# Order of ScalarE and VectorE in the compression stage, and where weight splits stand in it

## The chip, the cores and the metric

The kernel runs on one core of a Trainium2 chip. The metric is the device time of one execution in microseconds. TensorE (PE) does the matrix products, ScalarE (ACT) and VectorE (DVE) copy, split and combine, GpSimd (POOL) helps, and SyncE (SP) issues nearly all DMA transfers.

## The reference, cut to what matters

One layer of a hybrid decoder block: RMSNorm, one wide input projection, an mLSTM branch and a sparse attention branch (NSA), merged and projected out. All in float32, for 512 tokens of width 1024. The changed part is the compression of keys and values for the NSA branch, with the rotary embedding (rope) of keys and queries around it:

```python
def _compress(kv, pos_emb, w1, w2):
    idx = jnp.arange(n_cmp)[:, None] * CMP_STRIDE + jnp.arange(CMP_BLOCK)[None, :]
    blocks = kv[:, idx] + pos_emb[None, None, :, None, :]
    blocks = jnp.moveaxis(blocks, 3, 1).reshape(B, G, n_cmp, CMP_BLOCK * dk)
    return jax.nn.gelu(blocks @ w1) @ w2
...
kc = _compress(kvh(p["n_kc"]), cmp_pos_k[l], cmp_w1_k[l], cmp_w2_k[l])
vc = _compress(kvh(p["n_vc"]), cmp_pos_v[l], cmp_w1_v[l], cmp_w2_v[l])
ks = _partial_rope(kvh(p["n_ks"]), positions).transpose(0, 2, 1, 3)
kw = _partial_rope(kvh(p["n_kw"]), positions).transpose(0, 2, 1, 3)
```

The compressed keys and values serve one softmax, the keys `ks` and `kw` two others. `_compress` works on 31 blocks, a width of 2048 and a hidden layer of 128: small products with a chain of small steps between them.

## The kernel before, in words

Every float32 product is made of three: both operands are split into a rounded high part (type fp32r) and a remainder, and high x high, high x low and low x high are summed. `split` (line 122) is two instructions: ScalarE copies to the high part, VectorE subtracts for the remainder. For a weight tile of 128 x 1024 they are called wh (ScalarE) and wl (VectorE) in the profile, and its raw tile is wr (three buffers; four of wh and wl each).

The input projection is cut into jobs of 128 columns. A job (`cols`) is 24 matmuls of 128x512 into one PSUM bank, "pp", on the normalised input hTh, hTl; then its `post` function reads the bank. The class `Stream` (line 156) deals these matmuls out one at a time: `stream.step(n)` writes n of them into the program, `stream.run()` finishes one job. They are the fillers that keep TensorE at work while other chains go on. When a job starts, `fetch` calls `weights` for a job further on (the stream holds two ahead): the transfer of wr, and in the kernel before the split at once.

The compression stage comes after three big products and ahead of the attention blocks. Its jobs, in order: the keys and the values to compress (their `post` is `blocks(i)`, line 799), two key jobs for rope (`kpost`), the first query job (`queries(0)`), then gate jobs (`gate_ab`) mixed with further query jobs.

- `blocks(i)`: loads W1 in two halves (wr) and W2; ScalarE copies the bank to Z (one buffer); GpSimd adds the position to overlapping windows, giving Xr; Xr is split into X and W1 into "w1t" (keys) or "yb" (values). In the kernel before all of that is written right there.
- `hidden(i)`: 16 matmuls of W1 and X into a "ps" bank, then ScalarE and VectorE add its halves: "both".
- `activated(i, both)`: one small product with "twice", then the tanh form of gelu in six small steps on ScalarE and VectorE: "u".
- `compress_k`, `compress_v`: one small product with W2, and small copies to KC or VC.
- `rope_a`, `rope_b`, `keys`, `query_heads`: ScalarE copies the bank to "rh"; SP sends four strips of 8 rows of rh into "rot"; VectorE multiplies ra = bank x Ct, rot = rot x St, and adds. For keys, ScalarE and VectorE then split into "k" (four transfers copy the halves to the other partitions); for a query, into two tiles "Th". The first scores of attention are products of k and Th.

What sets the order: the program is written once in Python, and a scheduler then places instructions on each engine by its own estimate of when each can start. An engine named in the set `ordered` keeps the order of the program instead; TensorE isn't in it in this stage. In the kernel before `ordered` is empty from the first big product up to line 1011, where ScalarE and VectorE join it until the attention blocks begin. Buffers (wr, wh, wl, Z, banks) are released by semaphores that the framework adds.

## Time and profile before

| | us |
|---|---|
| median of 3 runs | 606.8 (605.92 to 607.37) |
| profiled execution, its own time | 607.47 |
| its span, first to last instruction | 605.4 |
| TensorE busy in the span | 591.8 |
| VectorE / ScalarE / GpSimd busy | 485.8 / 350.5 / 81.9 |
| granted TensorE clock, mean | 0.994 |

Lines of a timeline read: start in us, duration in us, engine, source line, operation, result <- operands, shapes, count; in square brackets how long the engine was idle before it, and what released it. Nearly all instructions carry line 80, where a helper records them, so they are told apart by the names of their tiles. The compression stage takes from about 174 us (the start of the first job, keys to compress) to 220 us (the first scores).

### The profile page before, as it was taken

Reading aid. Unit: us, or ns where it says so; the run is one execution under the profiler, and the core shown is the slowest. Engines: PE = TensorE matmul, PEld = TensorE weight load, DVE = VectorE, ACT = ScalarE, POOL = GpSimd, SP = SyncE. Lnnn points to the kernel's source line nnn. Section 1 sums busy time; section 2 is a strip of 40 time slices with the busy share of each in tenths; the row PEclk is TensorE's granted clock in tenths of the full one; section 3 lists DMA queues with packets and bytes.
Section 4 is the critical chain, followed back from the end, with each engine's and each line's share of the span. In section 5 each row is a group of like instructions: output and inputs, shape, how many; then the busy total and the mean of one; then the engine's idle time right before and its main releaser. Section 6 shows DMA issues by size and latency. Waiting matters only on the chain.

```text
span 605.4 us, 8474 instructions
## 1 busy us (share of the span) xinstructions
PE 591.8 (98%) x2956; PEld 496.6 (82%) x2956; DVE 485.8 (80%) x901; ACT 350.5 (58%) x645; POOL 81.9 (14%) x136
## 2 busy tenths in 40 slices
PE   7999999999999899999999999999999999999995
PEld 6988888888887788888888888888887878888885
DVE  5879889597686688887876866889989897589975
ACT  5855546654457366657666665657665653434564
POOL 3100000000005011414324230001010101010121
PEclk9999999999999899999999999999999999999998
DMA  7956654402046644313132214423133153890633
GB/s 222 337 173 178 204 169 128 150 2 87 18 114 177 152 121 125 106 40 106 39 88 68 72 53 123 139 71 88 53 98 110 39 171 110 281 265 24 209 53 139
DMA packets 86740, 74.17 MB, mean 123 GB/s; under 512 B 5229, under 2 KB 69353, under 8 KB 86698
## 3 DMA queue, kind: packets, MB, share of 16 engines
q1 hardware_dynamic: 85400, 70.94, 39.3%
q0 software_dynamic: 1008, 2.36, 2.1%
q8 instruction: 23, 0.38, 0.3%
q10 hardware_dynamic: 290, 0.33, 0.2%
q14 instruction: 19, 0.16, 0.1%
HBM read 61.36 MB, written 8.45 MB: 115 GB/s over the span
## 4 chain that ended last, share of the span: by engine, by line
PE 57%; DVE 6%; ACT 2%; issue 2%; POOL 1%; POOLq 0%; DVEq 0%; ACTq 0%
PE pp L80 39%; PE ps L80 9%; PE pt L80 5%; PE po L80 4%; DVE u L80 2%; DVE wl L80 1%; DVE xo L80 1%; ACT Dm L80 1%; ACT qkh L80 0%; POOL Xr L824 0%; POOL rho L1364 0%; ACT num L80 0%; DVE yal L80 0%; ACT wh L80 0%; DVE num L80 0%
## 5 line engine op out<-in xcount | busy, mean ns | idle before, releaser
L80 PE MATMUL pp<-hTl,wh 128*128 128x512 f32 x352 | 142.7, 405 | 0.0
L80 PE MATMUL pp<-hTh,wh 128*128 128x512 f32 x352 | 139.3, 396 | 0.0
L80 PE MATMUL pp<-hTh,wl 128*128 128x512 f32 x352 | 139.0, 395 | 0.0
L80 DVE TENSOR_TENSOR wl<-wr,wh 128x1024 fp32r<-128x1024 f32 x56 | 69.2, 1239 | 12.0 <-ACT wh L80 11.8
L80 ACT ACTIVATE wh<-wr 128x1024 fp32r<-128x1024 f32 x56 | 58.5, 1059 | 33.3 <-PE pp L80 23.0
L80 PEld LDWEIGHTS pp<-hTh,wh 128*128 128x128 f32 x352 | 66.4, 189 | 12.8
L80 PEld LDWEIGHTS pp<-hTl,wh 128*128 128x128 f32 x352 | 66.6, 189 | 10.6
L80 PEld LDWEIGHTS pp<-hTh,wl 128*128 128x128 f32 x352 | 66.6, 189 | 10.6
L80 ACT ACTIVATE P<-P,st 128x128 f32<-128x128 f32 (+3 forms) x64 | 35.7, 558 | 28.5 <-DVE st L80 28.3
L1110 POOL TENSOR_SCALAR P<-P,st 128x128 f32<-128x128 f32 (+3 forms) x56 | 38.0, 696 | 91.7 <-DVE st L80 59.0
L80 DVE TENSOR_TENSOR wl<-T,wh 128x1024 fp32r<-128x1024 f32 x28 | 34.0, 1222 | 11.3 <-ACT wh L80 11.2
L80 DVE TENSOR_TENSOR wl<-R,wh 128x1024 fp32r<-128x1024 f32 x28 | 33.9, 1222 | 10.2 <-ACT wh L80 10.2
L80 DVE TENSOR_TENSOR ptl<-pt,pth 128x512 fp32r<-128x512 f32 (+1 forms) x64 | 30.9, 485 | 12.2 <-ACT pth L80 11.6
L80 ACT ACTIVATE wh<-T 128x1024 fp32r<-128x1024 f32 x28 | 29.4, 1056 | 18.3 <-PE pp L80 11.0
L80 ACT ACTIVATE pth<-pt 128x512 fp32r<-128x512 f32 (+1 forms) x64 | 27.5, 429 | 20.3 <-PE pt L80 20.0
L80 DVE SCALAR_TENSOR_TENSOR u<-pp,prm,u 128x511 f32<-128x511 f32 (+2 forms) x48 | 35.7, 743 | 2.6 <-ACT u L80 2.3
L80 ACT ACTIVATE wh<-R 128x1024 fp32r<-128x1024 f32 x28 | 29.1, 1056 | 12.4 <-PE pp L80 5.3
L80 DVE CUSTOM_DVE_ANT_0 P<-ps,cst 128x128 f32<-128x128 f32 (+3 forms) x64 | 30.6, 484 | 5.5 <-PE ps L80 5.3
L80 PE MATMUL ps<-k,Th 128*128 128x256 f32 (+2 forms) x112 | 28.6, 336 | 0.0
L80 PE MATMUL pt<-cst,P 128*128 128x128 f32 x160 | 27.9, 272 | 0.0
L80 PEld LDWEIGHTS pt<-cst,P 128*128 128x128 f32 x160 | 20.8, 140 | 7.1 <-DVE ptl L80 0.3
L80 PE MATMUL pp<-yah,wh 128*128 128x512 f32 x64 | 25.0, 390 | 0.0
(355 smaller groups left out, 1360.8 us busy)
## 6 DMA issues: line engine op xcount, KB each, us to landing
wr<-w_in SPq DMA_DIRECT2D x44, 512.0 KB
R<-w_in SPq DMA_DIRECT2D x24, 512.0 KB
gD<-sg SPq DMA_DIRECT2D x16, 256.0 KB
s<-gD SPq DMA_DIRECT2D x16, 256.0 KB
wr<-w_branch_a SPq DMA_DIRECT2D x8, 512.0 KB
R<-w_out SPq DMA_DIRECT2D x8, 512.0 KB
vD<-cq SPq DMA_DIRECT2D x8, 256.0 KB
wr<-vD SPq DMA_DIRECT2D x4, 512.0 KB
```

The source lines that it names most:

```text
L80: ins = fn(*args, **kw)
L1110: pool.tensor_scalar(pj, pj, st[:, 2, j : j + 1], 1.0, OP.mult, OP.mult)
```

## The change

ScalarE and VectorE join `ordered` after the first job of the stage instead of near its end. From then on `weights` doesn't split at once: it puts the split into a queue, `pending`, and a call of `prepare()` between two groups of fillers writes the oldest one into the program. The splits of W1 and X move from `blocks` into a function `pack`, which is called for the keys after the value job and for the values after `hidden(0)`; within it W1 now comes ahead of X. The calls of the stage are spread anew over the fillers: 16 matmuls between most steps of the small chains, 8 or 4 at others. The value compression moves behind the first query's heads. The stage has as many jobs, products and transfers as before.

```diff
+    pending = deque()
+    lazy = []
+
+    def prepare():
+        pending.popleft()()
...
-        split(raw, hi, lo, eng)
+        if lazy:
+            pending.append(lambda: split(raw, hi, lo, eng))
+        else:
+            split(raw, hi, lo, eng)
         return hi, lo
...
-                side_by_side(raw.rearrange("p j g n -> p j (g n)"), X, js)
-            for raw, js in zip(raws, halves_of_j):
-                side_by_side(raw, W1[i], js)
+                blocked.append(raw.rearrange("p j g n -> p j (g n)"))
             Xs.append(X)
+
+            def pack():
+                for dst, srcs in ((W1[i], raws), (X, blocked)):
+                    for src, js in zip(srcs, halves_of_j):
+                        side_by_side(src, dst, js)
+
+            packs.append(pack)
...
-    stream.run(3)
+    stream.run()
+    ordered.update(("act", "dve"))
+    lazy.append(True)
+    stream.run()
+    packs[0]()
+    stream.step(8)
+    prepare()
+    stream.step(8)
     u0 = hidden(0)
+    packs[1]()
     stream.step(16)
+    prepare()
+    stream.step(8)
     u0 = activated(0, u0)
-    stream.run()
+    stream.step(8)
     keys(0, rope_b(*roped.pop(("k", 0))))
     u1 = hidden(1)
+    stream.step(8)
+    prepare()
     compress_k(u0)
-    stream.step(16)
-    u1 = activated(1, u1)
-    stream.run()
+    stream.step(4)
+    keys(1, rope_b(*roped.pop(("k", 1))))
+    stream.step(8)
+    u1 = activated(1, u1)
+    stream.step(4)
-    keys(1, rope_b(*roped.pop(("k", 1))))
-    compress_v(u1)
-    ordered.update(("act", "dve"))
     first = query_turned(0)
     stream.step(4)
     query_heads(0, first)
-    stream.step(PRE_FILL)
+    prepare()
+    stream.step(8)
+    compress_v(u1)
+    lazy.clear()
+    stream.step(12)
     ordered.clear()
+    prepare()
```

How the instructions stand on the engines is shown at three places. In the names a number tells buffers of one kind apart, and the two kernels number them differently.

First, ScalarE at the start of the stage. pp_1631 is the bank of the key job, pp_1690 (before) and pp_1680 (now) that of the value job. Before:

```order
L80 ACTIVATE w1t_1604<-wr_1656 128x8x128
L80 ACTIVATE w1t_1604<-wr_1658 128x8x128
L80 ACTIVATE Z_1662<-pp_1631 64x256 x4
L80 ACTIVATE wh_1686<-wr_1684 128x1024
L80 ACTIVATE X0_1667<-Xr_1668 128x8x64
L80 ACTIVATE X0_1667<-Xr_1674 128x8x64
L80 ACTIVATE yb_1592<-wr_1715 128x8x128
L80 ACTIVATE Z_1721<-pp_1690 64x256 x4
```

Now:

```order
L80 ACTIVATE Z_1662<-pp_1631 64x256 x4
L80 ACTIVATE Z_1711<-pp_1680 64x256 x4
L80 ACTIVATE w1t_1604<-wr_1656 128x8x128
L80 ACTIVATE w1t_1604<-wr_1658 128x8x128
L80 ACTIVATE X0_1667<-Xr_1668 128x8x64
L80 ACTIVATE X0_1667<-Xr_1672 128x8x64
L80 ACTIVATE wh_1678<-wr_1676 128x1024
L80 ACTIVATE both_1773<-ps_1756 128x128
```

The copies of the value job's bank moved ahead of the splits of the keys' W1 and X, and one weight split is left ahead of "both".

Second, ScalarE where the first query is turned: pp_1894 (before) and pp_1884 (now) are the query job's bank, wh_1964, wh_2019 and wh_2093 the weights of jobs ahead, wh_1882 those of the job after the next one. Before:

```order
L80 ACTIVATE u1_1913<-ps_1911 128x64
L80 ACTIVATE k00_1609<-ra_1850 64x512
L80 ACTIVATE u21_1914<-u21_1914 128x64
L80 ACTIVATE rh_1930<-pp_1894 128x512
L80 ACTIVATE k10_1611<-ra_1850 64x512
L80 ACTIVATE VC0_1584<-ps_1948 32x64 x2
L80 ACTIVATE VC1_1585<-ps_1948 32x64 x2
L80 ACTIVATE wh_1964<-wr_1962 128x1024
L80 ACTIVATE wh_2019<-wr_2017 128x1024
L80 ACTIVATE wh_2093<-wr_2091 128x1024
L80 ACTIVATE Th_1973<-ra_1936 64x512
L80 ACTIVATE Th_1976<-ra_1936 64x512
```

Now:

```order
L80 ACTIVATE k00_1609<-ra_1848 64x512
L80 ACTIVATE k10_1611<-ra_1848 64x512
L80 ACTIVATE u1_1925<-ps_1923 128x64
L80 ACTIVATE u21_1926<-u21_1926 128x64
L80 ACTIVATE rh_1938<-pp_1884 128x512
L80 ACTIVATE Th_1957<-ra_1944 64x512
L80 ACTIVATE Th_1960<-ra_1944 64x512
L80 ACTIVATE wh_1882<-wr_1880 128x1024
L80 ACTIVATE VC0_1584<-ps_1973 32x64
L80 ACTIVATE wh_1950<-wr_1948 128x1024
```

The second keys and both steps of u1 moved ahead of rh, and the weight splits and VC behind Th.

Third, TensorE at the first scores, ps_2010. Before (pp_2023 is the second job after the query job, 24 matmuls of the first, pp_1968, lie ahead of it, and 7 of its own lie ahead of these rows):

```order
L80 MATMUL pp_2031<-KC0_1582,rh_1930 128x64 x4
L80 MATMUL pp_2023<-hTl_78,wh_1890 128x512
L80 MATMUL pp_2023<-hTh_77,wl_1891 128x512
L80 MATMUL pp_2023<-hTh_77,wh_1890 128x512
L80 MATMUL pp_2023<-hTl_78,wh_1890 128x512
L80 MATMUL pp_2023<-hTh_77,wl_1891 128x512
L80 MATMUL pp_2023<-hTh_77,wh_1890 128x512
L80 MATMUL pp_2023<-hTl_78,wh_1890 128x512
L80 MATMUL ps_2010<-k00_1609,Th_1973 128x256
L80 MATMUL ps_2010<-k01_1610,Th_1973 128x256
```

Now (pp_1952 is the first job after the query job, and this is its last matmul):

```order
L80 MATMUL pp_1952<-hTh_77,wl_1803 128x512
L80 MATMUL ps_1973<-w2t1_1608,u1_1925 64x64
L80 MATMUL ps_2010<-k00_1609,Th_1957 128x256
L80 MATMUL ps_2010<-k01_1610,Th_1957 128x256
L80 MATMUL pp_2023<-hTh_77,wh_1882 128x512
L80 MATMUL pp_2023<-hTl_78,wh_1882 128x512
L80 MATMUL pp_2031<-KC0_1582,rh_1938 128x64 x3
```

Between the query job and the first scores there were 24 + 14 fillers, and there are 24; the value product moved from the middle of the job after the query to its end.

## The prediction

> **What bounds the kernel now.** I read the page first, its busy line and three rows of its 40 slices.

> ```profile
> PE 591.8 (98%) x2956; PEld 496.6 (82%) x2956; DVE 485.8 (80%) x901; ACT 350.5 (58%) x645; POOL 81.9 (14%) x136
> PE   7999999999999899999999999999999999999995
> PEclk9999999999999899999999999999999999999998
> ```

> TensorE is busy for 591.8 of 605.4 us. What an edit can win is the 13.6 us in which it is idle, and the time in which its clock is low. Start and end hold most of the idle time; between them one slice, the fourteenth (197 to 212 us), has an 8 for PE and an 8 for its clock. The windows view splits it (columns: us, busy time of PE, PEld, DVE, ACT, POOL with instruction counts, clock, DMA share, GB/s).

> ```profile
> 0.00:30.00 30.00, 26.41 (x170) 23.93 (x171) 20.90 (x35) 21.10 (x38) 7.27 (x21) 1.00 0.89 279
> 179.14:184.58 5.44, 5.44 (x26) 4.50 (x24) 3.67 (x3) 3.76 (x7) 3.42 (x3) 1.00 0.41 110
> 195.75:198.34 2.59, 0.00 (x1) 0.00 (x1) 2.53 (x4) 1.14 (x2) 0.00 (x0) 1.00 0.75 209
> 199.00:202.40 3.40, 3.40 (x11) 2.71 (x10) 2.20 (x7) 0.66 (x3) 0.00 (x0) 0.50 0.86 213
> 600.00:605.40 5.40, 0.00 (x0) 0.00 (x0) 0.87 (x3) 1.51 (x3) 0.55 (x1) 0.66 0.52 194
> ```

> The start costs 3.6 us and the last slice 5.4; the change touches neither. In the compression stage TensorE stands still for 2.59 us, and then runs for 3.4 us at half clock (0.50), which loses 1.7 us more. So the stage offers 2.6 + 1.7 = 4.3 us and no more. The second row is one filler job: 24 matmuls in 5.44 us, 0.227 us each. The timeline of VectorE and TensorE tells what held it up:

> ```profile
> 191.64 2.09 DVE L80 TENSOR_TENSOR X<-Xr,X 128x512 fp32r<-128x512 f32 x2
> 193.99 2.36 DVE L80 TENSOR_TENSOR wl<-wr,wh 128x1024 fp32r<-128x1024 f32 x2 [0.26 <-ACT wh L80]
> 196.87 1.22 DVE L80 TENSOR_TENSOR wl<-wr,wh 128x1024 fp32r<-128x1024 f32 x1
> 198.00 0.29 DVE L80 TENSOR_TENSOR both<-ps,both 128x128 f32<-128x128 f32 x1
> 198.34 0.43 PE L80 MATMUL ps<-twice,both 128*128 128x64 f32 x2 [2.59 <-DVE both L80]
> ```

> The addition for "both" (0.29 us) stands behind three weight splits of filler jobs. Nothing else is late in the stage: after 198.34 TensorE has no gap up to the attention blocks.

> **What the change removes.** With both engines in program order and each split postponed to the middle of the job ahead, "both" of key and value have one split ahead of them instead of three, and 16 fillers between. The 2.59 us gap should go: minus 2.6 us. How the low clock goes with it is weighed below.

> **What it adds, step by step.** I walk through the new order with durations of these rows (ScalarE and VectorE; "xN" rows are whole groups):

> ```profile
> 178.42 2.01 ACT L80 ACTIVATE w1t<-wr 128x1024 fp32r<-128x1024 f32 x2 [1.65 <-DVE gate L80]
> 179.52 2.36 DVE L80 TENSOR_TENSOR w1t<-wr,w1t 128x1024 fp32r<-128x1024 f32 x2 [1.03 <-ACT w1t L80]
> 180.34 1.55 ACT L80 ACTIVATE Z<-pp 64x256 f32<-64x256 f32 x4
> 184.58 0.39 PE L80 MATMUL pp<-hTh,wh 128*128 128x512 f32 x1
> 184.97 1.36 ACT L80 ACTIVATE X<-Xr 128x512 fp32r<-128x512 f32 x2 [2.00 <-POOL Xr L824]
> 185.64 1.42 DVE L80 TENSOR_TENSOR X<-Xr,X 128x512 fp32r<-128x512 f32 x2 [1.32 <-ACT X L80]
> 190.02 2.08 PE L80 MATMUL ps<-w1t,X 128*128 128x256 f32 x16
> 199.07 0.23 DVE L80 TENSOR_TENSOR u<-u 128x64 f32<-128x64 f32 x1 [0.78 <-ACT u L80]
> 199.82 0.26 ACT L80 ACTIVATE u<-u 128x64 f32<-128x64 f32 x1 [0.78 <-DVE u L80]
> 202.53 1.27 ACT L80 ACTIVATE k<-ra 64x512 fp32r<-64x512 f32 x2
> 203.27 1.39 DVE L80 TENSOR_TENSOR k<-ra,k 64x512 fp32r<-64x512 f32 x2
> 205.02 0.20 DVE L80 COPY KC<-ps 64x32 f32<-64x32 f32 x1
> 205.47 0.19 DVE L80 COPY KC<-ps 64x32 f32<-64x32 f32 x1 [0.26 <-ACT KC L80]
> 207.37 0.55 SPq L890 DMA_DIRECT2D k<-k  x1
> ```

> First hidden layer. Up to 184.6 us both kernels run the same matmuls without a gap. The Z copies of the value job now stand ahead of the splits of W1 and X, and wait for that job's last matmul, 184.8. Z 1.55 gives 186.3; the first half of w1t 187.4; VectorE's two w1t remainders 189.7; the first X remainder 190.4. TensorE comes there after 23 fillers, 184.58 + 23 x 0.227 = 189.8: it waits 0.6 us. (Bounds: 0 if the semaphores come a little earlier, 1.3 with the whole of X.)

> Second hidden layer. The hidden layer takes 1.9 us, then come 1 + 16 fillers, the small product (0.3) and 8 more: 198.3. VectorE has "both" by 193, two yb remainders by 196.2, X by 197.6: in time. W1 of the values is fetched later than now (its buffers come free with the w1t remainders, 188.6 and 189.7); at the 209 GB/s above a 512 KB transfer takes 2.5 us, so at worst it lands at 194.7 and X is late by 0.5 us. I take 0.

> Activation and keys. ScalarE's rh copy of the second key job waits behind the tanh of u (200.4), which waits for X, ra and a split on VectorE (199.4); it ends at 201.0. VectorE then does ra, rot, ra (3 x 0.69, to 203.1), ScalarE two k (to 204.4), "both" (204.7) and a split (205.8). TensorE, with 8 + 14 fillers behind it, needs "both" at 205.5: ready at 205.4. It ends the query job at 206.25, and its next job's third matmul (206.7) waits for the split's remainder, 205.8 + 1.22 = 207.0: 0.3 us. That job, the last one with weights ready, ends at 212.0. Meanwhile: copies of KC to 207.6, rot and ra of the second keys to 209.0, two k on ScalarE to 210.3, u to 210.5, VectorE's k remainder to 211.0 and u to 211.8, tanh 212.0, two small steps 212.4. The value product waits for them 0.4 us and ends at 212.7.

> The query's rope is the step that decides. It follows in the rows of the kernel before like this, for both key jobs and the query job:

> ```profile
> 194.93 0.60 ACT L80 ACTIVATE rh<-pp 128x512 f32<-128x512 f32 x1
> 200.00 0.69 DVE L80 TENSOR_TENSOR rot<-rot,St 128x512 f32<-128x512 f32 x1 [0.21 <-DMA rot<-rh]
> 202.03 0.60 ACT L80 ACTIVATE rh<-pp 128x512 f32<-128x512 f32 x1 [1.96 <-PE pp L80]
> 206.84 0.69 DVE L80 TENSOR_TENSOR rot<-rot,St 128x512 f32<-128x512 f32 x1 [1.18 <-DMA rot<-rh]
> 210.20 0.60 ACT L80 ACTIVATE rh<-pp 128x512 f32<-128x512 f32 x1
> 210.82 3.54 SPq L770 DMA_DIRECT2D rot<-rh  x4
> 215.81 0.69 DVE L80 TENSOR_TENSOR rot<-rot,St 128x512 f32<-128x512 f32 x1 [1.22 <-DMA rot<-rh]
> 217.27 1.28 ACT L80 ACTIVATE Th<-ra 64x512 fp32r<-64x512 f32 x2 [0.25 <-DVE ra L80]
> 218.40 1.40 DVE L80 TENSOR_TENSOR Th<-ra,Th 64x512 fp32r<-64x512 f32 x2
> 220.03 0.63 PE L80 MATMUL ps<-k,Th 128*128 128x256 f32 x4
> ```

> From the end of rh to the rot multiplication: 4.5, 4.2 and 5.0 us, four small transfers issued one after another by SP; VectorE waits for them each time. From rh's start to the first score: 9.8 us here, in which TensorE did 38 fillers, since the weights of two jobs were split ahead of Th. In the new order the split of the next job stands behind both Th on ScalarE, so TensorE has 24 fillers after the query job and then nothing: neither the score nor a filler can start. The rh copy itself stands behind the second keys and u's tanh: 212.0. SP issues the second keys' four transfers ahead of rot's (0.55 us each, the last after VectorE's k remainder at 211.0), and is free by 212.6. Then 0.6 for rh, transfers 4.5, rot and ra 1.4, Th 0.63, its remainder 0.69: 219.8. TensorE waits from 212.7: **7.1 us**. Bounds: the least is rh at the very end of the query job, with the shortest transfer: 0.6 + 4.2 + 1.4 + 1.3 = 7.5 us against 24 fillers, 5.44: 2.1 us. The most is this walk with transfers of 5.0 and 1 us more of queueing ahead: 8.6. I take the walk, because program order holds rh behind the tanh whatever the engines do. The next job's first matmul then waits for its split, which ends 1.06 us after the second Th, 220.75, against scores done at 220.3: 0.45 us.

> Sum of new waits: 0.6 + 0.3 + 0.4 + 7.1 + 0.45 = 8.85 us, against 2.59 removed: plus 6.25.

> Clock. The low clock of now began at 199.0, 3.25 us after TensorE stopped, and ended 4.1 us after it resumed. After 7.1 us of standing still it is certainly low at the restart; if it recovers as above, within 0.9 to 4.3 us after the restart, it loses half of that, 0.45 to 2.1. I take 1.5, so that 1.7 goes and 1.5 comes: minus 0.2. The small waits bring no low clock: no run of low clock but this and the end shows in the slices. [...]

> After the scores. The four small splits and two copies of VC, and two more weight splits, now fall into the first blocks of attention. VectorE has little room there:

> ```profile
> 213.24 0.29 DVE L80 CAST VC<-VC 64x256 fp32r<-64x256 f32 x1
> 213.56 0.22 DVE L80 TENSOR_TENSOR VC<-ps,VC 32x64 fp32r<-32x64 f32 x1
> ```

> ```profile
> 220.00:230.00 10.00, 10.00 (x53) 8.40 (x52) 9.69 (x32) 6.78 (x19) 2.61 (x3) 1.00 0.73 204
> ```

> They bring it some 3.9 us of work (two splits 2.4, VC 4 x 0.22 + 2 x 0.29 = 1.5). Bounds 0 to 3.9; I take 0, because the fillers of the next two jobs cover TensorE and its half clock gives VectorE time; the 3.9 is the upper end of the range.

> Total: 6.25 - 0.2 = about 6.0 us. The profiled execution took 607.47 us for a span of 605.4 (2.1 around it), so it becomes 613.5; the median of the three runs is 606.8, 0.7 below it, and becomes **612.8 us**.

> **The rivals.** (1) The gap goes and the rope hardly costs: 2.1 us of waiting, too little for the clock to fall, and 4.3 won: 606.8 - 2.2 = 604.6. For it: the earlier gap was 2.59 and small waits elsewhere leave the clock alone. Against it: it needs rh to start when the query job ends, while two k copies that hang on the second rope's transfers, and two steps of u behind them, stand ahead of it on ScalarE. It wins as soon as the wait for Th is under about 3 us. (2) It balances: a wait of some 4 us with its low clock costs what it saves, 605.6 to 608.0; for that the second keys would have to be done 3 us sooner than in my walk, for example if their transfers land under the split ahead. (3) The backlog of VC and splits stops TensorE in the attention blocks too: 612.8 + 3.9 = 616.7. For it, VectorE at 9.69 of 10; against it, the fillers. That the change does nothing can be left out: the order of both engines is another.

> **How the numbers follow.** Forecast 0.72; (1) 0.08; (2) 0.07; (3) 0.13. About 0.2% (1.2 us) is what a measurement of this kernel can tell from no change. Faster 0.09, the same 0.06, slower 0.85. The range goes from a wait of some 3.5 us with its clock (3.6 us less than the walk's 7.1: 609.2, and 0.7 less for the small waits: 608.5) to just under the third case: 616.5.

> **What would show it.** Right: no wait at "twice, both"; a gap of 5 to 8.5 us of TensorE ahead of the first product of k and Th, released by VectorE's Th, with rot's transfers in the chain of waits, and clock 0.50 right behind it. Wrong: the first score without a wait, or rh of the query job within a microsecond of that job's last matmul. If the gap is there and the time isn't up, my belief that TensorE's order can't make it good later is wrong.

## The result: 1.45% slower, and the profile after

The changed kernel takes 615.77 us (median, 614.8 to 616.19), the kernel before beside it 607.03. The ratio is 1.0145, with a 95% interval of 1.013 to 1.0161: 8.7 us slower, where the prediction had 6.0 and a range that ends at 616.5. The profiled execution took 614.8 us for a span of 612.8.

Of the page of the changed kernel, these are the busy line and TensorE's two rows of the 40 slices:

```profile
PE 594.2 (97%) x2956; PEld 497.3 (81%) x2956; DVE 486.2 (79%) x901; ACT 350.8 (57%) x645; POOL 82.8 (14%) x136
PE   8999999999999869999999999999999999999995
PEclk9999999999999979999999999999999999999999
```

The hole of the fourteenth slice is now in the fifteenth (a 6), with a 7 for the clock beside it. The first 176 us of an execution differ by up to 1.25 us from one profile to the next, so I compare a stretch rather than dates: from the start of ScalarE's last step on zt, ahead of the stage, to the first product of lf in the attention blocks. Where two kernels' dates are compared below, they too are counted from that step. In the windows view (length, then busy time of PE, PEld, DVE, ACT, POOL, clock, DMA share, GB/s) the kernel before has for it

```profile
176.14:262.25 86.11, 83.52 (x425) 69.92 (x425) 66.22 (x155) 53.70 (x119) 22.21 (x31) 0.98 0.49 127
```

and the changed kernel, with the part at low clock that follows the long wait as the second row,

```profile
175.16:269.54 94.38, 84.86 (x426) 70.20 (x425) 66.53 (x154) 53.36 (x119) 21.45 (x30) 0.96 0.44 116
...
220.11:224.77 4.66, 4.45 (x14) 3.67 (x15) 4.15 (x11) 4.24 (x10) 0.56 (x1) 0.50 0.26 63
```

So the stretch is 8.27 us longer. The profiled executions themselves differ by 7.3 us (614.80 and 607.47), since the part ahead of the stretch was 0.98 us shorter in the changed kernel's; the medians differ by 8.7. TensorE's idle time in it went from 2.59 to 9.52 us, plus 6.93. The low clock cost half of 3.41 us before (1.7) and half of 4.66 now (2.3), plus 0.6. The last 0.7 lies in TensorE's busy time at full clock, and I can't place it for certain. An estimate: a matmul is shown 0.39 us long while they follow each other 0.227 apart, so each wait may be some 0.16 us longer than it is shown; with six waits instead of one that would be 0.8 us.

TensorE's timeline of the changed kernel shows where it stands still:

```profile
190.47 1.78 PE L80 MATMUL ps<-w1t,X 128*128 128x256 f32 x13 [1.50 <-issue]
...
205.70 0.43 PE L80 MATMUL ps<-twice,both 128*128 128x64 f32 x2
...
213.19 0.30 PE L80 MATMUL ps<-w2t,u 128*64 128x64 f32 x2 [0.69 <-ACT rh L80]
220.11 0.80 PE L80 MATMUL ps<-k,Th 128*128 128x256 f32 x2 [6.62 <-DVE Th L80]
221.12 0.79 PE L80 MATMUL pp<-hTh,wh 128*128 128x512 f32 x1 [0.21 <-ACT wh L80]
...
234.81 0.60 PE L80 MATMUL pp<-cst,sc 128*64 128x128 f32 x4 [0.39 <-DVE sc L80]
```

The old wait at "twice, both" is gone. The first product of w1t and X waits 1.50 us, and the view names nothing that released it ("issue"); the run pack_first below shows that it waits for the splits of W1 and X. The first score waits 6.62 us, released by VectorE's Th. The chain ahead of it, from ScalarE's, SP's and VectorE's timelines of the changed kernel:

```profile
209.35 1.29 ACT L80 ACTIVATE k<-ra 64x512 fp32r<-64x512 f32 x2 [1.71 <-DVE ra L80]
...
212.19 0.26 ACT L80 ACTIVATE u<-u 128x64 f32<-128x64 f32 x1 [1.31 <-DVE u L80]
212.41 0.60 ACT L80 ACTIVATE rh<-pp 128x512 f32<-128x512 f32 x1
...
213.04 2.76 SPq L779 DMA_DIRECT2D rot<-rh  x4
...
217.26 0.69 DVE L80 TENSOR_TENSOR rot<-rot,St 128x512 f32<-128x512 f32 x1 [3.52 <-DMA rot<-rh]
...
218.71 1.28 ACT L80 ACTIVATE Th<-ra 64x512 fp32r<-64x512 f32 x2 [5.70 <-DVE ra L80]
220.01 1.06 ACT L80 ACTIVATE wh<-wr 128x1024 fp32r<-128x1024 f32 x1
```

rh stands behind the second keys' k and the tanh of u, although the query job's last matmul ended at 206.65. ScalarE then waits 5.70 us for the rope. The split of the next job (wh, 220.01) could have run in that time, but in program order it comes after Th.

### The profile page after: what moved, and what is told of

It is laid out like the page before. It is cut to its first block, busy times and chain, and to the rows that moved or that the text cites. A ratio compares the mean times of both kernels' runs of the same rounds, so it can differ in the third digit from the quotient of the medians.

```text
span 612.8 us, 8481 instructions
## 1 busy us (share of the span) xinstructions
PE 594.2 (97%) x2956; PEld 497.3 (81%) x2956; DVE 486.2 (79%) x901; ACT 350.8 (57%) x645; POOL 82.8 (14%) x136
## 3 DMA queue, kind: packets, MB, share of 16 engines
q0 software_dynamic: 1008, 2.36, 2.1%
## 4 chain that ended last, share of the span: by engine, by line
PE 81%; DVE 8%; ACT 4%; issue 2%; DMA 2%; POOL 1%; SPq 1%; POOLq 0%; DVEq 0%; ACTq 0%
PE pp L80 47%; PE ps L80 19%; PE pt L80 11%; PE po L80 4%; DVE u L80 2%; DVE wl L80 2%; DVE xo L80 1%; DMA xt<-x 1%; ACT Dm L80 1%; DMA wr<-cmp_w_v 1%; SPq L779 1%; DMA rot<-rh 1%; ACT wh L80 1%; ACT qkh L80 0%; POOL rho L1395 0%
## 5 line engine op out<-in xcount | busy, mean ns | idle before, releaser
L80 PE MATMUL pp<-hTl,wh 128*128 128x512 f32 x352 | 142.6, 405 | 0.0
L80 PE MATMUL pp<-hTh,wh 128*128 128x512 f32 x352 | 139.4, 396 | 0.2 <-ACT wh L80 0.2
L80 PE MATMUL pp<-hTh,wl 128*128 128x512 f32 x352 | 138.8, 394 | 0.1
L80 DVE TENSOR_TENSOR wl<-wr,wh 128x1024 fp32r<-128x1024 f32 x56 | 69.4, 1239 | 12.0 <-ACT wh L80 11.6
L80 ACT ACTIVATE wh<-wr 128x1024 fp32r<-128x1024 f32 x56 | 58.9, 1058 | 33.0 <-PE pp L80 26.6
L80 PEld LDWEIGHTS pp<-hTh,wh 128*128 128x128 f32 x352 | 66.5, 189 | 13.2 <-ACT wh L80 0.5
L80 PEld LDWEIGHTS pp<-hTh,wl 128*128 128x128 f32 x352 | 66.6, 189 | 10.9 <-DVE wl L80 0.6
L80 PEld LDWEIGHTS pp<-hTl,wh 128*128 128x128 f32 x352 | 66.6, 189 | 10.6
L80 ACT ACTIVATE P<-P,st 128x128 f32<-128x128 f32 (+3 forms) x64 | 35.7, 558 | 30.3 <-DVE st L80 30.2
L1141 POOL TENSOR_SCALAR P<-P,st 128x128 f32<-128x128 f32 (+3 forms) x56 | 39.7, 727 | 90.6 <-DVE st L80 65.3
L80 DVE TENSOR_TENSOR wl<-T,wh 128x1024 fp32r<-128x1024 f32 x28 | 34.0, 1222 | 12.4 <-ACT wh L80 12.3
L80 DVE TENSOR_TENSOR wl<-R,wh 128x1024 fp32r<-128x1024 f32 x28 | 33.8, 1220 | 10.4 <-ACT wh L80 10.4
L80 DVE TENSOR_TENSOR ptl<-pt,pth 128x512 fp32r<-128x512 f32 (+1 forms) x64 | 30.9, 485 | 12.6 <-ACT pth L80 11.9
L80 ACT ACTIVATE wh<-T 128x1024 fp32r<-128x1024 f32 x28 | 29.4, 1056 | 18.3 <-PE pp L80 11.0
L80 ACT ACTIVATE pth<-pt 128x512 fp32r<-128x512 f32 (+1 forms) x64 | 27.5, 429 | 19.2 <-PE pt L80 18.8
L80 DVE SCALAR_TENSOR_TENSOR u<-pp,prm,u 128x511 f32<-128x511 f32 (+2 forms) x48 | 35.6, 742 | 2.6 <-ACT u L80 2.3
L80 ACT ACTIVATE wh<-R 128x1024 fp32r<-128x1024 f32 x28 | 29.1, 1056 | 13.5 <-PE pp L80 6.4
L80 PE MATMUL ps<-k,Th 128*128 128x256 f32 (+2 forms) x112 | 29.0, 340 | 6.6 <-DVE Th L80 6.6
L80 DVE CUSTOM_DVE_ANT_0 P<-ps,cst 128x128 f32<-128x128 f32 (+3 forms) x64 | 30.5, 481 | 5.4 <-PE ps L80 5.2
L80 PE MATMUL pt<-cst,P 128*128 128x128 f32 x160 | 28.1, 272 | 0.0
L80 PEld LDWEIGHTS pt<-cst,P 128*128 128x128 f32 x160 | 20.8, 140 | 7.0 <-DVE ptl L80 0.3
L80 PEld LDWEIGHTS ps<-k,Th 128*128 128x128 f32 x112 | 19.0, 191 | 7.8 <-DVE Th L80 6.8
```

Source lines behind the costliest of these rows:

```text
L80: ins = fn(*args, **kw)
L1141: pool.tensor_scalar(pj, pj, st[:, 2, j : j + 1], 1.0, OP.mult, OP.mult)
```

## The experiments

Times are medians, with the ratio to the kernel before that ran beside them; "stretch" is the length defined above, and "idle" TensorE's idle time in it.

| kernel | us | ratio (95%) | stretch | idle |
|---|---|---|---|---|
| before | 605.7 to 607.2 | | 86.11 | 2.59 |
| changed | 615.77 | 1.0145 (1.0130 to 1.0161) | 94.38 | 9.52 |
| split_ahead | 609.89 | 1.0051 (1.0032 to 1.0071) | 87.82 | 4.43 |
| idle_matmuls | 613.90 | 1.0122 (1.0101 to 1.0143) | 92.46 | 3.27 |
| order_alone | 604.61 | 0.9957 (0.9942 to 0.9972) | 83.74 | 1.28 |
| no_order | 605.39 | 0.9975 (0.9963 to 0.9986) | 84.80 | 2.44 |
| pack_first | 612.36 | 1.0114 (1.0092 to 1.0135) | 91.33 | 6.20 |
| query_first | 613.53 | 1.0126 (1.0108 to 1.0144) | 92.72 | 7.09 |
| value_later | 605.93 | 0.9987 (0.9974 to 1.0000) | 85.12 | 1.97 |
| both_moved | 605.72 | 0.9993 (0.9982 to 1.0003) | 84.63 | 1.79 |
| behind_th | 604.84 | 0.9971 (0.9956 to 0.9986) | 83.97 | 1.52 |
| half_idle | 615.65 | 1.0152 (1.0128 to 1.0177) | 94.85 | 6.53 |
| next_behind_th | 610.84 | 1.0072 (1.0045 to 1.0098) | 90.07 | 4.61 |
| past_u | 604.09 | 0.9954 (0.9940 to 0.9969) | 83.17 | 0.80 |

**split_ahead: the next job's split ahead of the query's rope.** The changed kernel with

```diff
     stream.step(4)
+    prepare()
     first = query_turned(0)
     stream.step(4)
     query_heads(0, first)
-    prepare()
```

> The changed kernel with one call moved: the split of the job that follows the query job is issued ahead of the query's rope instead of behind both Th. Theory (the first score has no filler to cover the rope): those 24 fillers now run while the four transfers of rot, the rope and Th are done, so the 6.62 us wait at the first product of k and Th falls below 1.5 us, the 0.50 clock at 220 us is gone, at most 1 us of waiting for the split itself comes, and the time is 615.8 - 6.6 - 2.3 + 0.5 = about 607.4 (606 to 609). Rival A (program order itself holds both engines back, so that a wait taken away at one place comes up at the next): 612 to 616, with a new wait of over 4 us in the same 15 us. Rival B (the work left over for VectorE in the first attention blocks is what costs): the wait shifts behind the first scores, 611 to 615.

The long wait and the low clock are gone, and the stretch is 6.6 us shorter; the time is just above the range expected. Of the idle time that is left, 2.7 us lie ahead of the scores (first hidden layer 1.52, value product 0.67, the split itself 0.52); what is new lies behind them. In the timelines of TensorE, VectorE and GpSimd of this kernel:

```profile
223.92 0.40 PE L80 MATMUL ps<-k,Th 128*128 128x256 f32 x2
...
228.87 0.33 PE L80 MATMUL pt<-cst,P 128*128 128x128 f32 x1 [1.47 <-POOL P L1114]
...
224.79 1.23 DVE L80 TENSOR_TENSOR wl<-wr,wh 128x1024 fp32r<-128x1024 f32 x1
226.05 0.21 DVE L80 TENSOR_TENSOR VC<-ps,VC 32x64 fp32r<-32x64 f32 x1
...
227.23 0.14 DVE L80 RECIPROCAL st<-st 128x1 f32<-128x1 f32 x1
227.30 1.19 DVE L80 TENSOR_TENSOR wl<-wr,wh 128x1024 fp32r<-128x1024 f32 x1
...
227.71 1.11 POOL L1114 TENSOR_SCALAR P<-P,st,gates 128x128 f32<-128x128 f32 x1 [38.88 <-ACT wh L80]
```

The first transposes of P wait 1.47 us for GpSimd. Its step reads P, st and gates, and starts 0.34 us after the reciprocal of st, which stands on VectorE behind a weight split and pieces of VC (the view names a wh of ScalarE, which the step doesn't read). The step then takes 1.11 us beside the next split's wl, where the same step takes 0.45 us in the kernel before. This is the backlog of the prediction's third rival: it was hidden in the changed kernel while TensorE was late anyway, and came out once it wasn't. Rival B named the right work but not its size: it is 1.5 us of the 8.7, not the whole. Rival A fell, since no wait of over 4 us took the place.

**idle_matmuls and half_idle: what the low clock costs by itself.** The changed kernel with matmuls written in front of the first score, 26 or 12 of them:

```diff
     compress_v(u1)
+    ordered.add("pe")
+    idle = PT()
+    for n in range(26):
+        pe.matmul(idle, hTh[:, 0, 0:128], hTh[:, 1, :], start=True, stop=True)
+    ordered.discard("pe")
```

> The changed kernel with 26 matmuls more, whose result nobody reads, on TensorE between the value product and the first score: 26 x 0.227 = 5.9 us, which lie in the 6.62 us wait. The first score can start no sooner. Theory (the low clock behind the wait costs 2.3 us by itself): TensorE stands still for under 1.5 us, no slice of low clock behind it, and the time is 615.8 - 2.3 = 613.5 (612.8 to 614.3). Rival (the low clock is free, since VectorE or the weights set the pace behind the wait): 615.8, within 0.6.

> The changed kernel with 12 matmuls in the wait at Th instead of 26, so that about 0.47 + 14 x 0.227 = 3.65 us of standing still are left. So far waits up to 1.5 us had no low clock, 2.59 us one stretch of 3.41 us at 0.50, and 4.89, 5.01 and 6.62 us one stretch of 6.83 us each. Theory (low clock comes in steps of 3.41 us, of which a longer wait takes more): one stretch of 3.41 us, of which 0.5 to 1.7 us are lost: 613.9 + 1.1 = 615.0 (614.2 to 615.8). Rival (the length is always two steps once a wait passes some 3 us): 6.83 us and 2.3 us or more lost: 616 to 617.

With 26, TensorE's timeline has

```profile
213.76 6.21 PE L80 MATMUL pt<-hTh 128*128 128x512 f32 x26
220.44 0.50 PE L80 MATMUL ps<-k,Th 128*128 128x256 f32 x2 [0.47 <-DVE Th L80]
```

and the clock stays at 1.00. The score starts no sooner (44.98 us after the start of the stretch, 44.95 in the changed kernel), and yet the stretch is 1.92 us shorter and the time, 613.90, is where the theory had it: the low clock is a cost of its own, a little less than the 2.33 counted. With 12, in the timeline and in a window at the low clock,

```profile
220.95 0.79 PE L80 MATMUL ps<-k,Th 128*128 128x256 f32 x2 [3.66 <-DVE Th L80]
...
220.95:226.88 5.93, 5.71 (x18) 4.74 (x19) 4.15 (x11) 4.26 (x10) 0.56 (x1) 0.50 0.42 111
```

a wait of 3.66 us is followed by 5.93 us at half clock, 3.0 us lost, more than after 6.62 us. The time fell in the range of the theory, but for a wrong reason: the low clock lasted two steps (6.83 us, of which 0.9 fell into the wait), as the rival had it. The rival's time was 0.4 us too high.

**order_alone: program order without postponed splits.** The kernel before with

```diff
     stream.run(3)
+    ordered.update(("act", "dve"))
     u0 = hidden(0)
...
     compress_v(u1)
-    ordered.update(("act", "dve"))
     first = query_turned(0)
```

> The kernel before with one part of the change alone: ScalarE and VectorE in program order from the first hidden layer on; splits are issued when a job's weights are fetched, as before, and the rest of the stage is as before. Theory (not the order costs, but that the split of the next job was put behind Th): both splits stand ahead of Th, so no long wait at the first score; and the addition for both of the key stands ahead of the split fetched after it, so that the 2.59 us wait falls below 1 us with its low clock: 607.0 - 1.6 - 1.7 = 603.7 to 605.5. Rival A (program order itself costs): a wait of over 3 us at the rope of the query or of the second keys, 610 or more. Rival C (the 2.59 us are no order matter but the amount of split work in that stretch): 606.5 to 607.5.

It is 0.43% faster than before. From VectorE's and ScalarE's timelines of this kernel:

```profile
195.58 0.28 DVE L80 TENSOR_TENSOR both<-ps,both 128x128 f32<-128x128 f32 x1
195.78 1.21 DVE L80 TENSOR_TENSOR wl<-wr,wh 128x1024 fp32r<-128x1024 f32 x1
...
213.69 2.96 ACT L80 ACTIVATE wh<-wr 128x1024 fp32r<-128x1024 f32 x3
216.55 1.27 ACT L80 ACTIVATE Th<-ra 64x512 fp32r<-64x512 f32 x2
```

"both" stands behind one weight split instead of three, and its wait is 0.32 us instead of 2.59. Three splits stand ahead of Th, so the score has fillers and waits for nothing. Program order is not what made the change slow; on its own it takes away the old wait and its low clock.

**no_order: postponed splits without program order.** The changed kernel with

```diff
     stream.run()
-    ordered.update(("act", "dve"))
     lazy.append(True)
```

> The changed kernel without its program order for the stage (nor the one that the kernel before has around Th): postponed splits, packs and the closer steps alone, ScalarE's and VectorE's instructions arranged by the scheduler. Theory: the scheduler puts the split of the next job ahead of Th, so the first score has fillers ahead of it; some wait at both of up to 1.2 us stays; no low clock: 602.5 to 606. Rival D (postponing the splits costs by itself, whatever the order): a wait of over 4 us for a split or for Th, 611 or more.

This too is faster than before, by 0.25%. The scheduler puts a split between rh and Th, in ScalarE's timeline:

```profile
208.32 0.58 ACT L80 ACTIVATE rh<-pp 128x512 f32<-128x512 f32 x1
...
212.42 1.06 ACT L80 ACTIVATE wh<-wr 128x1024 fp32r<-128x1024 f32 x1 [0.42 <-PE pp L80]
...
218.35 1.28 ACT L80 ACTIVATE Th<-ra 64x512 fp32r<-64x512 f32 x2 [0.85 <-DVE ra L80]
```

From rh to Th it takes 10.0 us here, longer than in the changed kernel (6.3), and there is no wait at the first score. TensorE's idle time, 2.44 us, is nearly what it was before (2.59), but it is spread over waits of 1.01 us at most, and no low clock follows: that is what this half gains. So each half of the change gains; together they lose, because program order keeps the postponed split where it was written.

**behind_th and next_behind_th: is the split behind Th enough?** Both add the queue of postponed splits to the kernel of order_alone and use it around the query alone. In behind_th,

```diff
     first = query_turned(0)
+    lazy.append(True)
     stream.step(4)
+    lazy.clear()
     query_heads(0, first)
+    prepare()
```

> The kernel with program order alone, with one piece of the change more: the split of the job after the next is postponed behind both Th. It asks whether that piece is enough to make the long wait, or whether it takes the late rh too. In the run of program order alone rh starts at 207.36, and rot takes about 5 us from there, the rope 1.4 and Th 1.3: 215.1, and the split 1.06 more, 216.2; TensorE has fillers and the products of KC and rh up to about 215.2. Theory (it takes both: the late rh and the postponed split): a wait of about 1 us (0.5 to 2) there, no low clock, 604.6 + 1 = 605.6 (604.8 to 606.8). Rival (the postponed split alone makes the wait): over 3 us, with low clock, 609 or more.

There is no wait at the score (604.84 us), but the run does not answer the question: the split that it postpones is that of the job after the next, and TensorE kept the fillers of the next. next_behind_th takes the right one:

```diff
     compress_k(u0)
+    lazy.append(True)
     stream.step(16)
...
     query_heads(0, first)
+    prepare()
+    lazy.clear()
     stream.step(PRE_FILL)
     ordered.clear()
+    prepare()
```

> The kernel with program order alone, with the splits of the next two jobs behind the query job's successor postponed: the one for the job right after it behind both Th, as in the change. (In the run before this, the split postponed behind Th was one job further on, so that TensorE kept its fillers.) rh starts on time here, and the rope takes what it takes: rh at about 206.5, rot 5 us later, ra at 213, Th to 214.3, its remainder 215; TensorE has 24 fillers after the query job and is through near 211.5. Theory (the postponed split makes a wait by itself, the late rh makes it longer): a wait of 2.5 to 4.5 us at the first product of k and Th, low clock for one or two steps of 3.41 us, 604.6 - 0.5 + 3.5 + 2 = 609.6 (608 to 611.5). Rival (without the late rh there is no wait worth the name): under 1.5 us, no low clock, 604 to 606.

In ScalarE's and TensorE's timelines of next_behind_th, and a window at the low clock:

```profile
206.18 0.60 ACT L80 ACTIVATE rh<-pp 128x512 f32<-128x512 f32 x1 [0.69 <-PE pp L80]
...
214.54 1.28 ACT L80 ACTIVATE Th<-ra 64x512 fp32r<-64x512 f32 x2 [2.06 <-DVE ra L80]
215.84 1.06 ACT L80 ACTIVATE wh<-wr 128x1024 fp32r<-128x1024 f32 x1
...
215.94 0.62 PE L80 MATMUL ps<-k,Th 128*128 128x256 f32 x3 [3.74 <-DVE Th L80]
...
216.54:223.37 6.83, 6.44 (x21) 5.46 (x21) 4.52 (x13) 4.24 (x11) 0.46 (x1) 0.50 0.68 189
```

rh starts when the bank is ready (it waits for TensorE), and the score still waits 3.74 us, with 6.83 us at half clock behind it: the stretch is 6.3 us longer than order_alone's. So the postponed split makes a long wait by itself. What the late rh adds can't be read off exactly: 6.62 less 3.74 is 2.9 us, but VectorE does its VC work here ahead of rot, which the changed kernel does behind the scores:

```profile
210.96 0.21 DVE L80 TENSOR_TENSOR VC<-ps,VC 32x64 fp32r<-32x64 f32 x1
...
213.09 0.69 DVE L80 TENSOR_TENSOR rot<-rot,St 128x512 f32<-128x512 f32 x1
```

(VectorE's timeline of next_behind_th; rot has no bracket, so it waited for VectorE and not for its transfers.)

**query_first: the query's rope ahead of the second keys.** The changed kernel with

```diff
-    stream.step(4)
-    keys(1, rope_b(*roped.pop(("k", 1))))
-    stream.step(8)
+    stream.step(12)
     u1 = activated(1, u1)
...
     query_heads(0, first)
     prepare()
+    keys(1, rope_b(*roped.pop(("k", 1))))
```

> The changed kernel with the second keys moved behind the query's rope, Th and the split of the next job; all else as in the changed kernel. It asks how much of the wait at Th comes from rh being late (it starts at 212.41, 5.8 us after the query job's last matmul at 206.65), and how much from there being only 24 fillers. Theory: rh starts within 1 us of the end of the query job, the rope's transfers take 4 to 5 us as ever, Th is done near 214; TensorE runs out of fillers near 212.2, and waits 1.5 to 3 us for Th plus about 1 us for the split behind it, with no low clock or a short one: 615.8 - 3.5 - 1.7 = 610.6 (608.5 to 612.5). So lateness is the larger part, the missing fillers the rest. Rival A (the second keys, now later, hold the scores up in their turn): a wait of over 5 us at a product with k, 614 or more. Rival B (fillers alone are what matters): the wait stays at over 5.5 us.

It was above the range expected. ScalarE's and TensorE's timelines:

```profile
209.36 0.60 ACT L80 ACTIVATE rh<-pp 128x512 f32<-128x512 f32 x1
215.99 1.28 ACT L80 ACTIVATE Th<-ra 64x512 fp32r<-64x512 f32 x2 [6.03 <-DVE ra L80]
217.30 2.95 ACT L80 ACTIVATE wh<-wr 128x1024 fp32r<-128x1024 f32 x3
...
218.41 0.80 PE L80 MATMUL pp<-hTh,wh 128*128 128x512 f32 x1 [4.89 <-ACT wh L80]
```

rh is 3.5 us earlier than in the changed kernel, but still behind the tanh of u, where my sum had counted it as on time. And TensorE is now released by the split behind both Th, 2.4 us after the start of Th, where it was released by VectorE's Th, 1.4 us after it. So the wait ends only 2.2 us earlier, and the stretch is 1.7 us shorter. It lies between the theory and its rivals: no wait of over 5 us, but 4.89. Rival A shows in little: a product with k waits 0.53 us for the transfers of the second keys (227.57).

**pack_first and both_moved: the wait of the first hidden layer.** In pack_first the changed kernel has

```diff
+    packs[0]()
     lazy.append(True)
     stream.run()
-    packs[0]()
```

and both_moved has this and the edit of split_ahead.

> The changed kernel with one call moved: the splits of the key's W1 and X are issued ahead of the value job, and so ahead of its Z copies, instead of behind them. Theory: the 1.5 us wait at the first product of w1t and X falls below 0.3 us, because the 3.8 us that ScalarE waits for the value job's last matmul no longer stand ahead of X. What follows hangs on TensorE (both, u and the query's rh all come after its products), so that the gain is not given back at Th: 615.8 - 1.5 = 614.3 (613.3 to 614.9), and the wait at Th stays 6 to 7.5 us. Rival: the rope's chain on ScalarE and VectorE doesn't move with TensorE; the wait at Th grows by the same 1.5 us to about 8.1 and the time stays 615.8, within 0.5.

> The changed kernel with both moves: the split of the job behind the query ahead of the query's rope, and the key's splits ahead of the value job. Theory: the two waits add up: 609.9 - 1.5 = 608.4 (607.4 to 609.2), since the 1.47 us at the first transposes of P and the 0.5 to 0.7 us at the value product and the split stay. Rival C (the backlog of VectorE is what is left; 1.5 us earlier on both engines it is worked off in time): 604 to 606.5, faster than before.

Both gained more than expected. TensorE's timeline of pack_first:

```profile
187.50 2.08 PE L80 MATMUL ps<-w1t,X 128*128 128x256 f32 x16
...
216.67 0.80 PE L80 MATMUL ps<-k,Th 128*128 128x256 f32 x2 [5.01 <-DVE Th L80]
```

The first hidden layer doesn't wait, and the scheduler, which sees it ready sooner, puts it 8 fillers further forward. It starts 3.2 us earlier than in the changed kernel, and the whole chain behind it moves: rh by 3.7 us. So the wait at Th shrinks too, to 5.01 us, where I had it stay. The stretch is 3.0 us shorter. In both_moved the wait at the first transposes of P is 0.93 us instead of 1.47, and the 0.5 us that split_ahead waits for the split itself are gone. Rival C of that run comes nearest: its range holds the time, and the backlog is worked off in part, but the result, 605.72, can't be told from before.

**value_later and past_u: can order_alone be improved?** value_later moves the value product behind four fillers; past_u postpones one split past the chain of u, and issues it ahead of the ropes:

```diff
     compress_k(u0)
+    lazy.append(True)
     stream.step(16)
     u1 = activated(1, u1)
+    prepare()
+    lazy.clear()
     stream.run()
```

> The kernel with program order alone (before, with both engines in program order from the first hidden layer on) and the value product moved behind the four fillers that follow the query's rope, so that it does not wait 0.86 us for u on VectorE. Theory: that wait goes and nothing takes its place: 604.6 - 0.9 = 603.7 (603.0 to 604.3). Rival C (the four splits and two copies of VC, now among the first attention blocks, hold up the first softmax there, as they did in the run with the split ahead, where TensorE waited 1.47 us for GpSimd's P): 604.4 to 605.8, with a wait of some 1 us at the first transposes of P.

> The kernel with program order alone, with the split of the job behind the query's successor postponed only past the small chain of u (five small VectorE steps and the tanh), and issued ahead of the second keys' and the query's rope. Theory (postponing a split past a small chain pays as long as it stays ahead of the rope): the 0.86 us wait at the value product falls below 0.3 us, the first score still has its fillers, no low clock, 604.6 - 0.6 = 604.0 (603.3 to 604.8). Rival (the 0.7 us are given back at the next place where VectorE is late, the rope or the first softmax): 604.4 to 605.2, with a wait of 0.5 us or more behind 208 us that the run of program order alone doesn't have; or, if the split comes too late there as well, a wait for it of over 1 us.

value_later was 1.4 us longer in the stretch than order_alone: the wait at the value product went from 0.86 to 0.20 us, but 0.78 us come at a filler that waits for VectorE's sc, and 0.5 at two transposes of P. That is nearest to rival C of that run, which had 1 us at the transposes alone; the time, 605.93, is just above its range. past_u is the fastest of all, 604.09 us, 0.46% under before. Its timeline of TensorE has no wait at the value product (the row has no bracket), and one that order_alone didn't have:

```profile
205.37 0.30 PE L80 MATMUL ps<-w2t,u 128*64 128x64 f32 x2
...
223.09 0.33 PE L80 MATMUL pt<-cst,P 128*128 128x128 f32 x1 [0.34 <-POOL P L1095]
```

That is what the change was made of, used once: here a split stands behind a small chain and ahead of the rope, and costs nothing. That it gains on order_alone is not shown: the stretch is 0.6 us shorter, but the intervals of the two times overlap.

## Why the prediction was right, and by how much not

**The gap removed: right.** "both" no longer waits (205.70). Program order does it without the postponing (order_alone, 2.59 to 0.32 us), and the rest of the change does most of it without program order (no_order, 0.83 us).

**The query's rope decides: right in place and cause, and near in size.** The wait was 6.62 us for 7.1 in the walk, within its bounds of 2.1 and 8.6. rh started at 212.41; the walk has 212.0 on the clock of the profile before, that is 211.0 on the new one, whose stage starts 1.0 us sooner, and TensorE ran out of work 1.8 us later than in the walk too. The two slips offset each other, so that the size is nearer than the steps that lead to it. The reason given, no filler because the next job's split stands behind Th, is shown twice: undone, the wait goes (split_ahead), and done alone it comes (next_behind_th, which postpones the split of the job behind it as well). The sentence that "program order holds rh behind the tanh whatever the engines do" names only a part of it: with rh on time 3.74 us are left.

**Rivals 1 (604.6) and 2 (605.6 to 608.0): wrong.** The first needed a wait of under about 3 us, the second one of some 4; it was 6.62. That 2.1 us of standing still would leave the clock alone was an assumption: the profiles have no wait between 1.52 and 2.59 us. Even with rh on time it was 3.74 us in next_behind_th, with 3.4 us of clock. Without the VC work ahead of rot it might come near the 2.1 us of rival 1; that was not tried.

**Rival 3 (616.7) and the range: in part luck.** The measured 615.77 is 3.0 us above the forecast, and nearer to rival 3, but not for that rival's reason: behind the scores the one wait of TensorE is 0.39 us. The range holds the time because its upper end was set by that backlog. With the walk's own terms at their upper bounds (1.3 for 0.6, 8.6 for 7.1, 2.1 for 1.5) the sum would have been 615.6.

**First hidden layer: mis-sized.** 0.6 us expected, at most 1.3; it was 1.50. The step that failed is "VectorE's two w1t remainders 189.7": they were taken at the 2.36 us of the kernel before, and took 3.20. They overlap with the additions Xr of GpSimd. Narrow windows of the changed kernel's timeline show the instructions one by one:

```profile
186.18 0.78 POOL L834 TENSOR_TENSOR Xr<-Z,prm 128x248 f32<-128x248 f32 x1
186.57 1.48 DVE L80 TENSOR_TENSOR w1t<-wr,w1t 128x1024 fp32r<-128x1024 f32 x1 [9.06 <-ACT w1t L80]
...
186.90 1.78 POOL L834 TENSOR_TENSOR Xr<-Z,prm 128x248 f32<-128x248 f32 x1
187.97 1.80 DVE L80 TENSOR_TENSOR w1t<-wr,w1t 128x1024 fp32r<-128x1024 f32 x1
```

The timelines of the kernel before show the same, and I had passed over it: a remainder of 128x1024 took 1.23 us where it started ahead of the Xr and 1.73 where it started while one was running.

```profile
187.31 1.23 DVE L80 TENSOR_TENSOR yb<-wr,yb 128x1024 fp32r<-128x1024 f32 x1 [0.25 <-ACT yb L80]
...
188.15 4.19 POOL L824 TENSOR_TENSOR Xr<-Z,prm 128x248 f32<-128x248 f32 x4 [2.48 <-ACT Z L80]
...
189.99 1.73 DVE L80 TENSOR_TENSOR yb<-wr,yb 128x1024 fp32r<-128x1024 f32 x1 [1.45 <-ACT yb L80]
```

An Xr that doesn't start inside a remainder took 0.75 to 0.79 us. In the rows of the changed kernel the first remainder starts inside an Xr and ends 1.09 us after it; the last Xr starts inside that remainder and ends 0.63 us after it; the second remainder starts inside that Xr and again ends 1.09 us after it. In the traces of both kernels these two distances, 1.08 or 1.09 and 0.62 or 0.63 us, are the same wherever an Xr and a remainder of 128x1024 overlap in the stage. The two remainders took 1.48 and 1.80 us, 0.26 and 0.58 more than the 1.22 of the last yb remainder of the changed kernel (195.61), which no Xr overlaps; what in the overlap makes them longer is not shown.

**Clock: mis-sized.** 1.5 us expected, bounds 0.45 to 2.1; it was 2.3 in the profiled execution, outside them. The step "if it recovers as above" failed: it took the 3.41 us that the low clock lasted after the wait of 2.59, and in the profiles it lasted twice that after every longer wait. In the other three executions of the changed kernel the mean clock was 0.989 to 0.990, where the profiled one had 0.993, and their spans were 0.9 to 1.5 us longer. One step of 3.41 us at half clock takes 1.7 us, 0.003 of the span, so these had about one step more, an estimate. That the walk takes off 1.7 us for the shorter wait's low clock is right for an execution like the profiled one, since in order_alone that wait and its low clock went together (the last section shows that others had no such step).

**Small waits: right in sum.** Value product 0.69 for 0.4, split of the last ready job 0.12 for 0.3, the next job's split 0.21 for 0.45. A wait of 0.39 us at the product of sc (234.81) was not in the walk.

**Backlog behind the scores: taken at 0, right for this kernel and not for its neighbours.** Beside the 0.39 us nothing waits there. TensorE came 6.6 us late, which gave VectorE time; the half clock that the prediction counted on isn't needed for it, since in idle_matmuls the score comes as late, the clock is full, and no wait for the backlog appears either. With the wait gone the backlog costs 1.5 us (split_ahead), so the price that the prediction bounded by 3.9 is real, only covered.

In sum, the stretch grew by 8.3 us where the walk has 6.0: idle time 9.5 for 8.85, low clock 2.3 for 1.5, and 0.7 that no step has. The medians grew by 8.7; the profiled execution was the shortest of the four, and the others had the lower clock.

## What to carry to other kernels

When an engine is put in program order, look at what is written behind each instruction that waits long there, above all the preparation of the work that is meant to cover that wait: the split of the next fillers has to be issued ahead of the rope that they are to hide. Two edits that gain singly (0.43% and 0.25% here) can lose 1.45% together, so take an edit apart before it is given up. And in the profiles here a wait of TensorE of 2.6 us or more cost more than its length: add half of the low clock that followed, 1.7 us after 2.6 and 2.3 to 3.4 us after 3.7 to 6.6; it differs from one execution of a kernel to the next.
